# One hybrid block on one core: the adaLN sums in runs of sixteen products, eight buffers of raw weights

## The chip, the core and the metric

The kernel runs on one core of a Trainium2 chip. The metric is the device time of one execution in microseconds (us), from launch to end; lower is better. The engines are named as the profile names them: PE is TensorE, which multiplies matrices, and PEld its weight loads; DVE is VectorE, ACT ScalarE, POOL GpSimd; SP is SyncE, whose queue issues nearly all transfers, in order.

## What is computed

A single transformer-like block on 256 latent tokens and 256 context tokens of width 2048, in f32. Cut to what matters here:

```python
m_x = silu(c) @ ada_w + ada_b            # six vectors of 2048: shift1, scale1, gate1, shift2, scale2, gate2
m_c = silu(c_ctx) @ ada_w + ada_b
o_c, states = mix(rmsnorm(ctx) * (1 + m_c[1]) + m_c[0], zero states)   # w_in, then four recurrent mixers
o_x, _ = mix(rmsnorm(x) * (1 + m_x[1]) + m_x[0], states)
h = x + m_x[2] * o_x
h = h + m_x[5] * swiglu(rmsnorm(h) * (1 + m_x[4]) + m_x[3])
out = rmsnorm(h)
```

`mix` projects its input by `w_in` (2048 x 6816), runs four mixers (GLA, gated DeltaNet, a short gated convolution, RWKV-7), each forward and backward in chunks, and projects the result by `w_out`. The adaLN vectors 2, 3 and 4 (`gate1`, `shift2`, `scale2`) are needed only after the mixers. They are the sums that this case is about.

## The kernel before

**Order.** The program is written with a planner: each engine's order of instructions is laid out ahead of time from the order of the source, from costs that the planner assumes, and from priorities. Inside `with tc.high_priority()` an instruction is put ahead of the others as soon as the planner believes it is ready. On the chip each engine then takes its list strictly in that order. The units of the mixers stand in a hand-written list (`ORDER`, lines 41 to 44); lower-case tokens work on the context, upper-case ones on the latents.

**Stages of the span.** Up to about 159 us: norms, first adaLN vectors and an early part of the context's projection. 159 to about 1,100 us: mixers with their projections. Then `w_out`, the two SwiGLU matrices (to about 1,970 us) and the last norm.

**Projections in the mixers.** `proj` (line 596) makes one 128-column tile of `w_in` for 256 tokens. It goes in four parts (`hf`). Each part loads 128 x 512 numbers of `w_in` (256 KB) into a buffer `wraw`, splits them on ACT and DVE into a high half `wh` and a low half `wl` (`split`, line 253), and makes twelve products of 256 columns into the tile `big`, so 48 per call.

**The adaLN sums.** `ada_pieces` (line 285) makes the vector `ci` from 64 pieces (four blocks `j`, sixteen depth tiles `kt`) and a `finish`. A piece loads 256 KB of `ada_later` into a `wraw` and makes four products `ob<-wraw,sc`, of 32 columns of weights each, one for each quarter `g` of the output's partitions. In f32 a product is two passes of PE, so a piece is eight instructions in the trace. The three vectors' pieces and their three `finish` stand in a list `feed`. Each part `hf` of `proj` takes the first two entries (line 606), so a call of `proj` is mixed with eight pieces; 24 calls empty the list. Only the piece's load is at high priority; its products are not. The token `FF0` of `ORDER` runs what is left of the list.

**Buffers.** `wraw` has six buffers of 2 KB in each partition, used in turn by the loads of `w_in`, of `ada_later` and, later, of `w_out`, and by the row in `finish`. A load waits on SP's queue until the buffer six places earlier has been given back: after `wl` is made for one of `w_in`, after the four products for one of `ada_later`. `wh` and `wl` have three buffers each.

**Other tiles that the change touches.** `gdn` keeps the products of keys with keys in `gd_kk` (read in `front`) and of keys with queries in `gd_kq` (made and read in `mid`); `gla` keeps its transposed values in `gd_vt`. `short_conv` writes its result to `sc_y`, of two buffers, and `put_y` (line 886) makes the two halves `yH` and `yL` of it.

Of the kernel before, what the change touches and what calls it, by code (L numbers as in the profile page):

```python
# [16 lines left out]
P = 128  # L17
D = 2048
KT = D // P
# [156 lines left out]
def block_kernel(ctx: ExitStack, tc: tile.TileContext, x, cx, ada_first, ada_later, ada_b, w_in, w_early, w_out,  # L176
                 w_gu, w_down, final_g, consts, params, small, out):
    nc = tc.nc
# [9 lines left out]
    def mk(pool, shape, tag, bufs=None, dt=F32):  # L188
        pool = sub.get(tag[:3], pool) if pool is sub.get("mx") else pool
        return pool.tile(list(shape), dt, tag=tag, name=nm(tag), bufs=bufs)  # L190
# [10 lines left out]
    def tt(o, a, b, op, e=None):  # L201
        (e or V).tensor_tensor(out=o, in0=a, in1=b, op=op)  # L202
# [10 lines left out]
    def mm(o, l, r, start=True, stop=True):  # L213
        return TE.matmul(o, l, r, start=start, stop=stop)  # L214
# [7 lines left out]
    MUL, ADD, SUB, MIN, MAX = ALU.mult, ALU.add, ALU.subtract, ALU.min, ALU.max  # L222
# [4 lines left out]
    wpool = ctx.enter_context(tc.tile_pool(name="wpool", bufs=1))  # L227
# [17 lines left out]
    sc = mk(keep, [P, KT, 32], "sc")  # L245


    wp = [wpool, 512, 3, 6]

    def wraw():  # L250
        return mk(wp[0], [P, wp[1]], "wraw", wp[3])
# [33 lines left out]
    def ada_pieces(ci, bank_of, tmp):  # L285

        st = {}

        def piece(j, kt):
            if not st:  # L290
                st["ps"] = bank_of([P, 512])
            ps = st["ps"]
            with tc.high_priority():
                raw = wraw()
                rv = raw.rearrange("p (g c) -> p g c", g=4)
                r0 = (((ci - 2) * 4 + j) * KT + kt) * P
                nc.sync.dma_start(raw, ada_later[r0:r0 + P, :])
            for g in range(4):
                mm(ps[32 * g:32 * g + 32, j * P:(j + 1) * P], sc[:, kt, :], rv[:, g], kt == 0, kt == KT - 1)

        def finish():
            ps = st["ps"]
            row = wraw()
            if ci == 2:
                G.memset(row, 0.0)
                for g in range(4):
                    nc.sync.dma_start(row[32 * g:32 * g + 1, :], ada_b[0:1, ci * D + g * 512: ci * D + (g + 1) * 512])
                tt(row, ps, row, ADD)
                for g in range(4):
                    nc.sync.dma_start(gate_dram[0:1, g * 512:(g + 1) * 512], row[32 * g:32 * g + 1, :])  # L310
                return
            acopy(row, ps)
            pt = bank_of([P, 4, 4, 32])
            for b in range(4):
                TE.transpose(pt[:, b].rearrange("p a c -> p (a c)"), row[:, b * P:(b + 1) * P], ident)
            t = modB if ci == 3 else modA
            tt(t[:, 2, :].rearrange("p (g b) -> p g b", b=4), pt[:, :, :, 0].rearrange("p b g -> p g b"),
               pc("adab", ci * 16, 16).rearrange("p (g b) -> p g b", b=4), ADD)
            if ci == 4:
                stt(t[:, 2, :], t[:, 2, :], 1.0, pc("n2g", 0, 16), ADD, MUL)  # L320

        return [lambda j=j, kt=kt: piece(j, kt) for j in range(4) for kt in range(KT)] + [finish]

    def rstd_of(src, tmp, n):
        junk = mk(tmp, [P, D], "junk", 1)
# [60 lines left out]
    with ExitStack() as st:  # L386
# [93 lines left out]
        for i in range(1, NE):  # L480
            n, k = EARLY[i - 1]
# [30 lines left out]
    with mix:  # L512
# [83 lines left out]
        def proj(nHL, which):  # L596

            r0 = TIDX[which] * P
            H, L = nHL
            ps = PB([P, T], "big")  # L600
            for hf in range(4):
                with tc.high_priority():
                    raw = wraw()
                    nc.sync.dma_start(raw, w_in[r0:r0 + P, hf * 512:(hf + 1) * 512])
                    wh, wl = split(raw, V)
                for f in feed[:2]:
                    f()
                del feed[:2]
                for k in range(4):
                    kt = hf * 4 + k  # L610
                    a, b = wh[:, k * P:(k + 1) * P], wl[:, k * P:(k + 1) * P]
                    mm(ps, a, H[kt], kt == 0, False)
                    mm(ps, a, L[kt], False, False)
                    mm(ps, b, H[kt], False, kt == KT - 1)
            return ps

        def pcol(nHL, name, i):
            return proj(nHL, (name, i))

        def t1(tag, bufs=1):  # L620
            return mk(mx, [P, T], tag, bufs)
# [264 lines left out]
        def put_y(i, y):  # L886
            if not yt:
                A.dma_start(Y[i], y)
                parked.append(i)
                return  # L890
            acopy(yt[0][i], y)
            tt(yt[1][i], y, yt[0][i].bitcast(F32), SUB)
# [199 lines left out]
        def gdn(h, s, raw, sm):  # L1092
# [29 lines left out]
            def front():  # L1122
                cur[0] = "b"
                com.update(raw())
                k = cvs(com["k"], 1, "gd_k")
                v = cvs(com["v"], 2, "gd_v")
                l2(k, 1.0)
                tok = mk(mx, [P, 4, P], "gd_tok", 2)
                pt = PB([P, 4, P])
                for c in range(2):  # L1130
                    TE.transpose(pt[:, c], k[:, c * P:(c + 1) * P], ident)
                    TE.transpose(pt[:, 2 + c], v[:, c * P:(c + 1) * P], ident)
                acopy(tok, pt)
                pk = PB([P, 2, P])
                for c in range(2):
                    sl = slice(c * P, (c + 1) * P)
                    mm(pk[:, c], k[:, sl], k[:, sl])
                kk = mk(mx, [P, 2, P], "gd_kk", 1)
                V.tensor_copy(kk, pk)

                pbc = decays()
                dl = mk(mx, [P, 4, P], "gd_dl", 2)
                for d in range(2):
                    for c in range(2):
                        cs = sm["cum"][:, d, h, c:c + 1]
                        V.scalar_tensor_tensor(out=dl[:, d * 2 + c], in0=pbc[:, d, c * P:(c + 1) * P], scalar=cs,
                                               in1=dlm[d], op0=SUB, op1=SUB)
                act(dl, dl, AF.Exp, scale=-1.0)
                for d in range(2):
                    for c in range(2):  # L1150
                        u = d * 2 + c
                        stt(dl[:, u], kk[:, c], sm["nb"][:, d, h, c:c + 1], dl[:, u], MUL, MUL)
                com.update(kn=k, tok=tok, nL=dl, Xc=small_inverses(dl, lowers))

            def mid():
                cur[0] = "b"
                tok = com["tok"]
                R = com["R"] = mk(mx, [P, 4, 2, P], "gd_R", 1)
                for d in range(2):
                    for c in range(2):  # L1160
                        u = d * 2 + c
                        ts(R[:, u, 0], tok[:, c], sm["kes"][:, d, h, c:c + 1], MUL, e=G)
                if s == 0:
                    return
                k = com["kn"]
                q = cvs(com["q"], 0, "gd_q")
                l2(q, P ** -0.5)
                pk = PB([P, 2, P])
                for c in range(2):
                    sl = slice(c * P, (c + 1) * P)  # L1170
                    mm(pk[:, c], k[:, sl], q[:, sl])
                kq = mk(mx, [P, 2, P], "gd_kq", 1)
                V.tensor_copy(kq, pk)
                pbc = decays()
                for d in range(2):
                    for c in range(2):
                        cs = sm["cum"][:, d, h, c:c + 1]
                        stt(R[:, d * 2 + c, 1], pbc[:, d, c * P:(c + 1) * P], cs, atm[d], SUB, ADD)
                act(R[:, :, 1], R[:, :, 1], AF.Exp)
                qe = com["qe"] = mk(mx, [P, 2, T], "gd_qe", 1)  # L1180
                act(qe, pbc, AF.Exp)
                tt(qe, qe, bcast(q, 1, 2), MUL, e=G)
                for d in range(2):
                    tt(R[:, 2 * d:2 * d + 2, 1], kq, R[:, 2 * d:2 * d + 2, 1], MUL)
# [72 lines left out]
        def gla(p, s, raw, sm):  # L1257
# [18 lines left out]
            else:  # L1276
# [4 lines left out]
                for c in range(2):  # L1281
                    for hh in range(2):
                        TE.transpose(pt[:, c * 2 + hh], v[:, c, hh], ident)
            vt = mk(mx, [P, 4, P], "gd_vt", 1)
            V.tensor_copy(vt, pt)
            for d in range(2):
                pz = PB([P, T])
# [84 lines left out]
        def short_conv(t, nHL):  # L1372
            cc_ = t1("xs", 2)
            acopy(cc_, pcol(nHL, "c_c", t))
            pr = t1("xs", 2)
            tt(pr, pcol(nHL, "c_h", t), cc_, MUL)
            o = cc_
            conv(o, pr, [pc("scconv", tap * 4 + t) for tap in range(3)], 1)
            yo = t1("sc_y", 2)
            tt(yo, pcol(nHL, "c_b", t), o, MUL)  # L1380
            put_y(8 + t, yo)

        def rw(p, s):
            def raw():
# [291 lines left out]
```

## Time and profile before

| | us |
|---|---|
| median of 3 runs (1997.1 to 2002.27) | 2000.33 |
| the profiled execution, its own time | 1993.64 |
| its span, from first to last instruction | 1991.9 |
| PE busy in the span | 1896.2 |
| DVE busy | 1356.5 |
| ACT busy | 1023.8 |

The profiled execution is 6.7 us below the median, and its own time is 1.7 us over its span. PE's busy time counts each instruction from its start to the end of its results, and successive products overlap; what a product costs in a stream is read from the start of one to the start of the next.

### The profile page before, as it was taken

Reading aid. Unit: us, or ns where it says so; the run is one execution under the profiler, and the core shown is the slowest. Engines: PE = TensorE matmul, PEld = TensorE weight load, DVE = VectorE, ACT = ScalarE, POOL = GpSimd, SP = SyncE. Lnnn points to the kernel's source line nnn. Section 1 sums busy time; section 2 is a strip of 40 time slices with the busy share of each in tenths; the row PEclk is TensorE's granted clock in tenths of the full one; section 3 lists DMA queues with packets and bytes.
Section 4 is the critical chain, followed back from the end, with each engine's and each line's share of the span. In section 5 each row is a group of like instructions: output and inputs, shape, how many; then the busy total and the mean of one; then the engine's idle time right before and its main releaser. Section 6 shows DMA issues by size and latency. Waiting matters only on the chain.

```text
span 1991.9 us, 36160 instructions
## 1 busy us (share of the span) xinstructions
PE 1896.2 (95%) x13312; PEld 1624.0 (82%) x13312; DVE 1356.5 (68%) x3327; ACT 1023.8 (51%) x2125; POOL 160.0 (8%) x207
## 2 busy tenths in 40 slices
PE   5998999999999999999999998999999999999997
PEld 3776777787878888888998977888888888888886
DVE  4446856898877789899767566996555555555554
ACT  2225645566565555566455555455555555544443
POOL 0002000000001000101001001111001010000000
PEclk9999999999999999999999999999999999999999
DMA  8976685444367432222244665896555555565554
GB/s 347 403 302 214 218 264 186 128 129 153 98 207 230 146 106 67 91 77 74 93 160 146 211 189 183 291 323 229 187 189 183 189 186 185 202 210 192 194 196 149
DMA packets 162081, 374.66 MB, mean 188 GB/s; under 512 B 17896, under 2 KB 43752, under 8 KB 156784
## 3 DMA queue, kind: packets, MB, share of 16 engines
q1 hardware_dynamic: 156288, 368.21, 53.9%
q10 hardware_dynamic: 5616, 4.14, 0.7%
q8 instruction: 104, 1.70, 0.4%
q14 instruction: 73, 0.60, 0.1%
HBM read 360.48 MB, written 11.80 MB: 187 GB/s over the span
## 4 chain that ended last, share of the span: by engine, by line
PE 79%; DVE 10%; ACT 5%; DMA 4%; issue 2%; POOL 0%; SPq 0%; ACTq 0%; DVEq 0%; POOLq 0%
PE acc L214 40%; PE big L214 15%; PE la L214 6%; PE ea L214 5%; PE lb L214 4%; DVE wl L202 3%; PE eb L214 3%; PE ob L214 3%; ACT wh L197 2%; DMA wraw<-in_w_in 1%; DMA wraw<-in_ada_later 1%; PE pt L214 0%; ACT rw_z L193 0%; DVE ivaXc L202 0%; DVE ivaw L202 0%
## 5 line engine op out<-in xcount | busy, mean ns | idle before, releaser
L202 DVE TENSOR_TENSOR wl<-wraw,wh 128x512 fp32r<-128x512 f32 x856 | 569.2, 691 | 390.5 <-ACT wh L197 382.4
L197 ACT ACTIVATE wh<-wraw 128x512 fp32r<-128x512 f32 x856 | 510.0, 626 | 508.3 <-PE acc L214 193.9
L214 PE MATMUL acc<-n,wh 128*128 128x512 f32 x1408 | 494.1, 400 | 3.1 <-ACT wh L197 3.1
L214 PE MATMUL acc<-n,wl 128*128 128x256 f32 x1408 | 382.6, 282 | 0.3 <-DVE wl L202 0.3
L214 PE MATMUL big<-nh,wh 128*128 128x256 f32 x1056 | 315.9, 300 | 3.7 <-ACT wh L197 2.9
L214 PE MATMUL big<-nh,wl 128*128 128x256 f32 x1056 | 310.9, 295 | 1.3 <-DVE wl L202 1.3
L214 PEld LDWEIGHTS acc<-n,wh 128*128 128x128 f32 x1408 | 260.4, 189 | 59.6 <-ACT wh L197 3.4
L214 PE MATMUL big<-nl,wh 128*128 128x256 f32 x1056 | 306.8, 291 | 0.0
L214 PEld LDWEIGHTS acc<-n,wl 128*128 128x128 f32 x1408 | 268.2, 190 | 9.8 <-DVE wl L202 1.2
L214 PEld LDWEIGHTS big<-nh,wh 128*128 128x128 f32 x1056 | 199.7, 189 | 22.2 <-issue 12.5
L214 PEld LDWEIGHTS big<-nh,wl 128*128 128x128 f32 x1056 | 199.7, 189 | 7.8 <-issue 3.1
L214 PEld LDWEIGHTS big<-nl,wh 128*128 128x128 f32 x1056 | 199.8, 189 | 3.5 <-issue 2.9
L214 PE MATMUL acc<-wl,hH 128*128 128x512 f32 x352 | 137.2, 390 | 0.3 <-DVE wl L202 0.2
L214 PE MATMUL acc<-wh,hH 128*128 128x512 f32 x352 | 137.4, 390 | 0.0
L214 PE MATMUL acc<-wh,hL 128*128 128x512 f32 x352 | 137.0, 389 | 0.0
L214 PE MATMUL ob<-wraw,sc 128*32 128x128 f32 x1536 | 85.9, 286 | 10.8 <-DMA wraw<-in_ada_later 7.2
L202 POOL TENSOR_TENSOR hL<-sg,hH 128x256 fp32r<-128x256 f32 x44 | 47.4, 1078 | 451.3 <-ACT hH L197 451.3
L214 PEld LDWEIGHTS acc<-wl,hH 128*128 128x128 f32 x352 | 66.1, 188 | 15.1 <-DVE wl L202 1.4
L214 PEld LDWEIGHTS acc<-wh,hH 128*128 128x128 f32 x352 | 66.1, 188 | 13.9 <-ACT up L197 0.2
L214 PEld LDWEIGHTS acc<-wh,hL 128*128 128x128 f32 x352 | 66.1, 188 | 13.8
L214 PEld LDWEIGHTS ob<-wraw,sc 128*32 128x32 f32 x1536 | 39.0, 110 | 37.3 <-DMA wraw<-in_ada_later 11.2
L202 DVE TENSOR_TENSOR wl<-wr,wh 128x1408 fp32r<-128x1408 f32 x16 | 26.0, 1623 | 42.9 <-ACT wh L197 42.9
(483 smaller groups left out, 3169.3 us busy)
## 6 DMA issues: line engine op xcount, KB each, us to landing
wraw<-in_w_gu SPq DMA_DIRECT2D x174, 512.0 KB, 3.4
wraw<-in_w_in SPq DMA_DIRECT2D x264, 256.0 KB, 3.0
wraw<-in_ada_later SPq DMA_DIRECT2D x256, 256.0 KB, 4.0
wraw<-in_w_down SPq DMA_DIRECT2D x88, 512.0 KB, 4.2
ad<-in_ada_first SPq DMA_DIRECT2D x32, 1024.0 KB, 10.3
wraw<-in_w_out SPq DMA_DIRECT2D x64, 256.0 KB, 2.8
wr<-in_w_early SPq DMA_DIRECT2D x16, 704.0 KB, 6.2
xin<-in_cx SPq DMA_DIRECT2D x2, 1024.0 KB
```

Source lines behind the costliest of these rows:

```text
L197: A.activation(o, i, AF.Copy)
L202: (e or V).tensor_tensor(out=o, in0=a, in1=b, op=op)
L214: return TE.matmul(o, l, r, start=start, stop=stop)
```

## The change

The four pieces of four successive depth tiles become one entry, `run`. It first asks for all four loads, that of its first depth tile last, then lists the sixteen products (32 instructions), these now at high priority too. `proj` takes one entry at its first and third part, so it is still mixed with eight pieces. `feed` has 51 entries in place of 195. `wraw` has eight buffers. Room for the two more comes from sharing: `gd_kk`, `gd_kq` and `gd_vt` become one tile of 2 KB, the first two as its halves, and the short convolution's last product is written over its input in place of `sc_y`.

```diff
-    wp = [wpool, 512, 3, 6]
+    wp = [wpool, 512, 3, 8]
...
-        def piece(j, kt):
+        def run(j, k0):
+
             if not st:
                 st["ps"] = bank_of([P, 512])
-            ps = st["ps"]
+            ps, raws = st["ps"], {}
+            for kt in (k0 + 1, k0 + 2, k0 + 3, k0):
+                with tc.high_priority():
+                    raws[kt] = wraw()
+                    r0 = (((ci - 2) * 4 + j) * KT + kt) * P
+                    nc.sync.dma_start(raws[kt], ada_later[r0:r0 + P, :])
             with tc.high_priority():
-                raw = wraw()
-                rv = raw.rearrange("p (g c) -> p g c", g=4)
-                r0 = (((ci - 2) * 4 + j) * KT + kt) * P
-                nc.sync.dma_start(raw, ada_later[r0:r0 + P, :])
-            for g in range(4):
-                mm(ps[32 * g:32 * g + 32, j * P:(j + 1) * P], sc[:, kt, :], rv[:, g], kt == 0, kt == KT - 1)
+                for kt in range(k0, k0 + 4):
+                    rv = raws[kt].rearrange("p (g c) -> p g c", g=4)
+                    for g in range(4):
+                        mm(ps[32 * g:32 * g + 32, j * P:(j + 1) * P], sc[:, kt, :], rv[:, g], kt == 0, kt == KT - 1)
...
-        return [lambda j=j, kt=kt: piece(j, kt) for j in range(4) for kt in range(KT)] + [finish]
+        return [lambda j=j, k0=k0: run(j, k0) for j in range(4) for k0 in range(0, KT, 4)] + [finish]
...
-                for f in feed[:2]:
-                    f()
-                del feed[:2]
+                if hf % 2 == 0:
+                    for f in feed[:1]:
+                        f()
+                    del feed[:1]
...
-                kk = mk(mx, [P, 2, P], "gd_kk", 1)
+                kq = mk(mx, [P, 4, P], "gd_kq", 1)
+                kk = kq[:, 0:2]
...
-                kq = mk(mx, [P, 2, P], "gd_kq", 1)
+                kq = com["kq"][:, 2:4]
...
-            vt = mk(mx, [P, 4, P], "gd_vt", 1)
+            vt = mk(mx, [P, 4, P], "gd_kq", 1)
...
-            yo = t1("sc_y", 2)
-            tt(yo, pcol(nHL, "c_b", t), o, MUL)
-            put_y(8 + t, yo)
+            tt(o, pcol(nHL, "c_b", t), o, MUL)
+            put_y(8 + t, o)
```

## Rows read from the trace of the kernel before

**Rows 1.** The page, chain that ended last, by engine.

```profile
PE 79%; DVE 10%; ACT 5%; DMA 4%; issue 2%; POOL 0%; SPq 0%; ACTq 0%; DVEq 0%; POOLq 0%
```

**Rows 2.** Stretches: start:end, length, busy us (PE, PEld, DVE, ACT, POOL), clock, DMA share, GB/s.

```profile
161.00:163.00 2.00, 2.00 (x17) 1.76 (x20) 0.56 (x1) 0.92 (x2) 2.00 (x9) 0.50 0.79 217
...
170.00:300.00 130.00, 123.48 (x1268) 99.06 (x1268) 90.59 (x294) 72.44 (x158) 12.62 (x17) 1.00 0.76 246
300.00:400.00 100.00, 90.68 (x752) 72.61 (x750) 72.67 (x229) 55.29 (x135) 6.24 (x12) 0.93 0.49 154
400.00:575.00 175.00, 170.59 (x1486) 146.18 (x1486) 148.97 (x500) 106.66 (x243) 14.84 (x25) 1.00 0.42 134
575.00:627.00 52.00, 50.55 (x537) 38.27 (x536) 40.07 (x130) 27.45 (x63) 3.49 (x6) 1.00 0.79 259
627.00:1100.00 473.00, 454.07 (x3450) 421.08 (x3449) 392.28 (x1121) 270.99 (x593) 47.92 (x62) 1.00 0.33 110
```

**Rows 3.** Tile ob: count, ns min/median/max, first and last start.

```profile
L214 PE MATMUL ob<-wraw,sc x1536: 272/273/423, 159.6 to 626.4; 128*32 128x128 f32 x192
```

**Rows 4.** PE's timeline around one piece: start us, length, what.

```profile
186.93 0.28 PE L214 MATMUL big<-nh,wl 128*128 128x256 f32 x1
...
187.14 0.43 PE L214 MATMUL ob<-wraw,sc 128*32 128x128 f32 x8
187.50 0.39 PE L214 MATMUL big<-nh,wh 128*128 128x256 f32 x1
187.72 0.28 PE L214 MATMUL big<-nl,wh 128*128 128x256 f32 x1
```

**Rows 5.** PE's timeline around two pieces on end.

```profile
165.21 0.27 PE L214 MATMUL big<-nh,wl 128*128 128x256 f32 x1
165.41 0.64 PE L214 MATMUL ob<-wraw,sc 128*32 128x128 f32 x16
165.99 0.39 PE L214 MATMUL big<-nh,wh 128*128 128x256 f32 x1
166.21 0.28 PE L214 MATMUL big<-nl,wh 128*128 128x256 f32 x1
```

**Rows 6.** PE's timeline: the longest run, and one quarter of a piece.

```profile
576.92 1.29 PE L214 MATMUL ob<-wraw,sc 128*32 128x128 f32 x38
...
617.60 0.41 PE L214 MATMUL ob<-wraw,sc 128*32 128x128 f32 x2
617.94 0.70 PE L214 MATMUL eb<-gd_sq,ones 128*128 128x256 f32 x2
```

**Rows 7.** Waits, 155 to 630 us: who for whom, us in all, times, longest.

```profile
PE ob L214 <- DMA wraw<-in_ada_later: 7.2, 14, 2.4
...
SPq L297 <- PE ob L214: 102.4, 69, 11.7
SPq L604 <- PE ob L214: 58.0, 35, 23.2
```

**Rows 8.** SP's timeline: first and fifth load of w_in, eight of ada_later between.

```profile
250.92 0.37 SPq L604 DMA_DIRECT2D wraw<-in_w_in  x1
...
261.21 0.33 SPq L604 DMA_DIRECT2D wraw<-in_w_in  x1
```

**Rows 9.** The page, DMA issues: count, KB each, median us to landing.

```profile
wraw<-in_w_in SPq DMA_DIRECT2D x264, 256.0 KB, 3.0
wraw<-in_ada_later SPq DMA_DIRECT2D x256, 256.0 KB, 4.0
```

**Rows 10.** Tiles gd_vt and sc_y: instructions, ns min/median/max, first and last start.

```profile
L1285 DVE COPY gd_vt<-eb x4: 679/690/692, 395.6 to 1069.3; 128x512 f32<-128x512 f32 x4
...
L202 DVE TENSOR_TENSOR yL<-sc_y,yH x4: 418/419/426, 1068.9 to 1133.5; 128x256 fp32r<-128x256 f32 x4
```

**Rows 11.** PE's timeline: the first two runs; in brackets idle time before, and releaser.

```profile
159.57 0.64 PE L214 MATMUL ob<-wraw,sc 128*32 128x128 f32 x16 [3.50 <-ACT h_d_k L197]
...
162.76 1.08 PE L214 MATMUL ob<-wraw,sc 128*32 128x128 f32 x16
```

More of the change, by code (lines that the diff above doesn't have):

```diff
@@ L1152, in front @@
                         stt(dl[:, u], kk[:, c], sm["nb"][:, d, h, c:c + 1], dl[:, u], MUL, MUL)
-                com.update(kn=k, tok=tok, nL=dl, Xc=small_inverses(dl, lowers))
+                com.update(kq=kq, kn=k, tok=tok, nL=dl, Xc=small_inverses(dl, lowers))
             def mid():
```

## The prediction

> **What bounds the kernel now.** I read the page's chain first: PE holds 79% of the path that ended last [rows 1]. Then the span by stretches [rows 2]. The adaLN products start between 159.6 and 626.4 us [rows 3], so the change acts there, and there PE is busy for 91 to 98% of the stretches while DVE is busy for 70 to 85%. The reader should see two kinds of stretch. In 170 to 300 and 575 to 627 us the transfer engines are busy for 0.76 and 0.79 of the time; in 300 to 575 us for 0.42 to 0.49. I call them dense and thin. Third, PE's timeline, from the start of one product to the start of the next, because busy time hides the price of a switch between kinds of products. Last, the waits of SP's queue [rows 7]: loads stood 102.4 + 58.0 us for a buffer that adaLN products had not yet given back. PE itself stood only 7.2 us for adaLN data.
>
> **Price of a run of adaLN products.** Two projection products follow each other in 0.12 us: in [rows 4] one lies between the row at 186.93 and the eight. From 186.93 to 187.72 us there is one piece of eight instructions and two steps of the stream. 0.79 less 2 x 0.12 is 0.55 us for the piece. With two pieces on end [rows 5], 165.21 to 166.21 less 0.24 gives 0.76 us. So the second piece costs 0.21 to 0.22 us, and 0.33 us of the first is the price of going to the narrow products and back. The longest row bears this out: 38 instructions last 1.29 us against 0.43 for eight, 0.23 per further eight [rows 4, 6]. A quarter of a piece, two instructions, holds PE from 617.60 to 617.94, 0.34 us, where a whole piece holds it 0.36 [rows 4, 6]: a cut inside a piece costs as much as one between pieces.
>
> **How many runs.** Along PE's timeline, from the first start in [rows 3] to the last, I counted the unbroken runs of the 1,536 instructions: 165. 105 have two to eight instructions (57 whole pieces, 48 fragments), 59 have ten to sixteen, one has 46 (the 38 of [rows 6] and eight more). At 0.55, 0.77 and 0.55 + 5 x 0.22 = 1.65 us that is 57.8 + 45.4 + 1.7 = 104.9 us of PE's time, without waits. After the change there are 48 runs of 32 instructions: 0.55 + 3 x 0.22 = 1.21 us each, 58.1 us in all. **PE has 46.8 us less to do.** This takes the runs to be unbroken. I take that, since all sixteen products are urgent and the first cannot start before the last load; broken once each they would cost 48 x 0.33 = 16 us more.
>
> **What of it reaches the end.** The 192 pieces lie 117 in the dense stretches, 159 to 300 and 575 to 627 us, and 75 in the thin ones. By the same count the dense ones save 22 us of PE, the thin ones 25.
>
> Thin, 300 to 575 us: PE was busy 261 of 275 us, DVE 222 [rows 2]. With 25 us less DVE would stand at 222 / 250 = 0.89, against 392 / 473 = 0.83 in the stretch behind it, where PE is still 96% busy [rows 2]. So DVE does not become the bound outright, but chains through DVE will show more often. Bounds: nothing (chains take it all) to 25 us. I take 20, four fifths, nearer to the upper end because of that later stretch.
>
> Dense: a projection and its eight pieces need twelve loads of 256 KB, 3.15 MB. Before, one such round took 261.21 - 250.92 = 10.3 us [rows 8]. PE needs 48 x 0.12 + 2 x 1.21 = 8.2 us after the change. The transfer engines moved 246 GB/s at a share of 0.76 and 259 at 0.79 [rows 2], so some 325 GB/s if they were never idle, an estimate from these rows: 9.7 us for the round. So transfers, not PE, limit the gain to 0.6 us in each of 117 / 8 = 14.6 rounds, 9 us. Bounds: 22 us, if other work of the mixers spreads the loads; a loss, if the buffers are the limit. Eight buffers hold two thirds of a round. The run gives back four at a stroke; the last two loads of the next run go out after that, land 4.0 us later [rows 9], and the run takes some 1.0 us from its first start: with 0.7 us for two issues [rows 8] 5.7 us a half, 11.4 a round, 1.1 us over 10.3 and 16 us in 14.6 rounds. With 3.0 us to landing, as for `w_in` [rows 9], it is 9.4. I take 10 us of gain.
>
> **Other edits.** The wait on a load now stands before sixteen products, and behind it on PE's list are the projection's products and the mixers' chains. The loads themselves are as many and as large; a run's four go out together ahead of the next part's `w_in`, whose twelve products wait for it through ACT and DVE. That is in the round above. `gd_kk` and `gd_kq` are written and read by DVE alone, in its own order, so sharing adds nothing there. `gd_vt` is read by PE: the four copies into it [rows 10] keep their place, and at most two of the DeltaNet units behind a GLA unit must wait for its last product. The order puts the projections of other units between; uncovered it is a copy's length, 0.7 us, twice. The short convolution's result now holds its buffer until `yL` is made, 0.42 us by DVE [rows 10] and about as much by ACT, four times: 3.4 us if nothing covered it, at 1,067 us and later, where other products fill PE. I cost these at nothing and keep 5 us for the range. In the `w_out` and SwiGLU stages the loads and products stay the same, so I cost two more buffers at nothing there.
>
> **Sum.** 20 + 10 = 30 us off the profiled execution's 1993.6 gives 1963.6. That execution lies 6.7 us under the median of the runs, so against the median it is **1970 us**, 1.5% faster. About 0.3%, 6 us, is what a measurement of this kernel can tell from no change.
>
> **The rivals.** *All of it arrives.* The full 46.8 us, and part of the waits at narrow products: 1953 us, and 1940 if some 13 us of loads' waits go too. For it: SP's 160 us behind adaLN products, and the two added buffers. Against it: the share of 0.76 to 0.79. Chance 0.17.
>
> *Buffers still bind.* The dense stretches give nothing or lose up to 10, the thin ones 15: 1985 to 1995 us. For it: the 11.4 us round. Chance 0.19, of which 0.07 is no measurable change.
>
> *Slower: PE stands before each run.* PE takes its list in order; where the planner believes four loads landed before they have, PE stands with everything behind it. A piece waits for one load, a run for the last of four. It decides at 46.8 / 48 = 0.98 us per run. At 1.5 us the time is 2000 + 48 x 1.5 - 46.8 = 2025 us. For it: a load takes 4.0 us [rows 9], and the dense stretches leave little slack. Against it: the 14 waits came to 0.5 us each [rows 7], and eight buffers let the plan ask earlier. Chance 0.06.
>
> *The clock.* From 161 to 163 us the granted clock was 0.50, the lower of its two levels, 1.2 GHz [rows 2]. PE had stood 3.5 us before 159.57, and a run of sixteen that lasts 0.64 us at full clock lasted 1.08 [rows 5, 11]. If longer waits ahead of each run brought this back, 48 runs of some 1.08 us would each take 1.08 x 0.44 / 0.64 = 0.74 us more: 36 us returned, and 1990 us or more. Against it: the clock is 1.00 in both dense stretches, waits included [rows 2]. Chance 0.03, 0.02 of it no change or a small gain, 0.01 slower. The Trainium skill, "TensorE: Matmul & The Clock Gate", section "HAM oscillation — how this bites in real kernels", speaks against this change: where short groups of products alternate with waits for data, the array falls back to its slow rate each time. By that rule the time is this rival's, by the rows the sum's; the trace agrees only in that the clock fell in stretches with waits.
>
> **How the numbers follow.** The forecast, 1955 to 1985 us, has 0.55; everything arriving 0.17; buffers binding 0.19; PE standing 0.06; the clock 0.03. Faster by over 0.3%: 0.55 + 0.17 + 0.12 + 0.01 = 0.85. Within 0.3%: 0.07 + 0.01 = 0.08. Slower: 0.06 + 0.01 = 0.07. The range runs from 1942, inside "all of it arrives", to 1994, the edge of no change; it leaves out about 0.05 below and 0.14 above.
>
> **What would show it.** The timeline after should have some 48 runs of 32 instructions, each about 1.0 us from its first start to the next product; fragments of two or six would show the first step wrong. Waits of PE for `ada_later` should stay near 7 us; above 40 the third rival holds. SP's waits for adaLN products should fall under 160 us. The dense stretches' share should rise towards 0.85, with a round near 9.7 us; a round over 10.3 shows that the buffers bind. The span behind 627 us should be as long as before, within 5 us. A replanned order that lengthens the mixers' chains anywhere from 159 to 1,100 us would make the sum wrong without any of these terms being so.

## The result, and the profile after

The changed kernel takes **1976.78 us** in the median of four runs (1975.5 to 1979.17), against 2001.3 for the kernel before in the same comparison: ratio **0.988**, 95% interval 0.9861 to 0.99. That is 24.5 us faster. The forecast was 1970, 30 us faster, in a range of 1942 to 1994. The profiled execution of the changed kernel took 1979.17 us, at the upper end of its runs, and that of before 1993.64, under all of its runs, so the two traces show 14.5 us of the 24.5.

PE's timeline of the changed kernel around one run (start, length, what):

```profile
184.20 1.08 PE L214 MATMUL ob<-wraw,sc 128*32 128x128 f32 x32
185.22 0.38 PE L214 MATMUL big<-nh,wh 128*128 128x256 f32 x1
185.44 0.28 PE L214 MATMUL big<-nl,wh 128*128 128x256 f32 x1
```

Thirty-two instructions in 1.08 us; [rows 4, 5] gave 0.43 + 3 x 0.22 = 1.09. Along the timeline there are 44 such runs and two of 64, in place of 165. Priced as in the prediction they cost 44 x 1.21 + 2 x 2.09 = 57.4 us, 47.5 less than before. The page shows what the trace has of that; PE's busy time and the chain by engine, after:

```profile
PE 1858.0 (94%) x13312; PEld 1622.9 (82%) x13312; DVE 1352.5 (68%) x3327; ACT 1020.7 (52%) x2125; POOL 155.0 (8%) x207
...
PE 75%; DVE 9%; DMA 8%; ACT 5%; issue 2%; POOL 0%; SPq 0%; ACTq 0%; DVEq 0%; POOLq 0%
```

PE is busy 1896.2 - 1858.0 = 38.2 us less, and its idle time grew from 1991.9 - 1896.2 = 95.7 to 1977.4 - 1858.0 = 119.4 us, by 23.7. The difference is the 14.5 us. Busy time falls by less than the price said. Taken in each trace from the start of the product ahead of a run to the start of the one behind it, less PE's idle time and one step of 0.12 us, the 165 runs come to 94 us and the 46 to 56, which is 37 less. So the prices of the pieces, 104.9 us in all, were some 11 us too high. The chain's share of DMA doubled against [rows 1].

To see where, I cut both traces at the same amount of other work: at the 1,100th, 2,000th, 3,400th and 3,800th of PE's products other than `ob<-wraw,sc`. The kernel before reaches the last three at 320.5, 556.1 and 631.6 us, the changed one at 323.5, 547.8 and 615.7; the tables start 18.3 us behind the 1,100th. The stretches between, first of before, then of after (start:end, length, busy us of PE, PEld, DVE, ACT and POOL, clock, DMA share, GB/s):

```profile
167.00:320.50 153.50, 146.43 (x1470) 117.59 (x1469) 109.66 (x361) 84.66 (x188) 15.05 (x23) 1.00 0.73 235
320.50:556.00 235.50, 222.26 (x1906) 186.84 (x1905) 190.92 (x625) 139.66 (x325) 17.07 (x30) 0.97 0.44 139
556.00:631.60 75.60, 74.08 (x738) 58.60 (x739) 57.90 (x181) 42.75 (x94) 6.38 (x9) 1.00 0.70 229
```

```profile
170.50:323.50 153.00, 136.00 (x1526) 119.91 (x1527) 110.19 (x358) 87.89 (x203) 10.65 (x19) 0.99 0.79 257
323.50:547.80 224.30, 207.09 (x1947) 185.77 (x1947) 185.36 (x594) 129.62 (x301) 17.57 (x32) 0.98 0.48 152
547.80:615.70 67.90, 62.09 (x627) 55.87 (x626) 54.57 (x164) 42.37 (x94) 5.22 (x8) 0.97 0.63 199
```

The first, dense stretch is as long as before: PE has 10.4 us less to do in it and stands 9.9 us longer. The thin one is 11.2 us shorter, the last 7.7. The sums themselves also moved forward: from the 3,400th to the 3,800th product PE does 336 of their 1,536 instructions before and 224 after, 14 pieces fewer, and more of them in both stretches ahead. So the last stretch's 7.7 us are in part only work done earlier. Ahead of the change's place the traces differ by 3.5 us the other way (the 1,100th product at 148.7 and 152.2 us), and behind it the changed kernel loses 2 us up to the 7,500th.

Waits from 155 to 630 us, after (who for whom, us in all, times, longest), against [rows 7]:

```profile
PE ob L214 <- DMA wraw<-in_ada_later: 21.2, 21, 2.9
...
SPq L608 <- PE ob L214: 45.3, 27, 23.5
...
SPq L298 <- DMA wraw<-in_ada_later: 28.2, 21, 3.3
...
SPq L298 <- PE ob L214: 24.6, 48, 1.9
```

PE stands 21.2 us for adaLN loads in place of 7.2. SP's waits for adaLN products fell from 160.4 to 69.9 us, and those put down to the adaLN loads themselves rose from 7.5 to 44.1.

The chain that ended last, within the first of these stretches, before and after:

```profile
by line: PE big L214 30.1%; PE ob L214 13.0%; DMA wraw<-in_w_in 9.3%; PE la L214 7.9%; DMA wraw<-in_ada_later 6.7%; PE eb L214 4.3%; PE lb L214 4.1%; PE ea L214 3.6%; DVE wl L202 2.2%; ACT wh L197 2.1%; issue 1.4%; PE ea L993 1.4%; DVE smd 
```

```profile
by line: DMA wraw<-in_ada_later 40.1%; PE big L214 21.1%; PE ob L214 13.3%; DMA wraw<-in_x 5.6%; PE la L214 4.1%; DVE wl L202 2.2%; PE lb L214 1.6%; PE eb L214 1.6%; issue 1.5%; DVE ivbw L202 1.3%; PE ea L214 1.3%; DVE ivbXc L202 1.3%; ACT 
```

So after the change two fifths of that stretch, 61 us in 13 places of 3.9 to 5.8 us, lie in adaLN loads on the path, against 7% before.

The four runs shown start 5.7 us apart on average (PE's timeline). They are among the closer ones: from 171.7 to 322.0 us 22 runs start, and the median step is 6.3 us, 12.6 for a round of two runs.

```profile
177.83 1.08 PE L214 MATMUL ob<-wraw,sc 128*32 128x128 f32 x32
...
184.20 1.08 PE L214 MATMUL ob<-wraw,sc 128*32 128x128 f32 x32
...
189.66 1.08 PE L214 MATMUL ob<-wraw,sc 128*32 128x128 f32 x32
...
194.88 1.08 PE L214 MATMUL ob<-wraw,sc 128*32 128x128 f32 x32
```

From the first load of `w_in` to the fifth, as in [rows 8], the kernel before has ten rounds that begin from 163.9 to 285.4 us: 10.3 to 21.4 us, median 12.2. The 10.3 of [rows 8] is the shortest of them. The changed kernel has ten from 164.0 to 275.9: 10.3 to 17.3 us, median 11.9.

### The profile page after: what moved, and what is told of

Read it like the earlier page. It is cut to its first block, busy times and chain, and to the rows that moved or that the text cites. A ratio compares the mean times of both kernels' runs of the same rounds, so it can differ in the third digit from the quotient of the medians.

```text
span 1977.4 us, 36172 instructions
## 1 busy us (share of the span) xinstructions
PE 1858.0 (94%) x13312; PEld 1622.9 (82%) x13312; DVE 1352.5 (68%) x3327; ACT 1020.7 (52%) x2125; POOL 155.0 (8%) x207
## 4 chain that ended last, share of the span: by engine, by line
PE 75%; DVE 9%; DMA 8%; ACT 5%; issue 2%; POOL 0%; SPq 0%; ACTq 0%; DVEq 0%; POOLq 0%
PE acc L214 40%; PE big L214 14%; PE la L214 6%; DMA wraw<-in_ada_later 5%; PE ea L214 5%; PE lb L214 3%; DVE wl L202 3%; PE eb L214 3%; PE ob L214 2%; ACT wh L197 2%; PE pt L214 0%; DMA wraw<-in_x 0%; DMA xin<-in_cx 0%; ACT rw_z L193 0%; DMA wraw<-in_w_in 0%
## 5 line engine op out<-in xcount | busy, mean ns | idle before, releaser
L214 PE MATMUL big<-nh,wh 128*128 128x256 f32 x1056 | 311.9, 296 | 4.4 <-ACT xs L197 3.0
L214 PE MATMUL ob<-wraw,sc 128*32 128x128 f32 x1536 | 52.7, 280 | 24.9 <-DMA wraw<-in_ada_later 21.2
L202 DVE TENSOR_TENSOR wl<-wr,wh 128x1408 fp32r<-128x1408 f32 x16 | 26.0, 1624 | 43.3 <-ACT wh L197 43.3
```

## The experiments

Each is the changed kernel with one edit, timed against the kernel before on the same chip. Theory A: the gain is fewer switches, and what is missing was lost to the runs' loads. Theory B: what is missing was lost to the mixers' own chains (or, in the first run, the gain is the two buffers).

**Parts of the change.** Old pieces, eight buffers, sharing kept:

```diff
-        def run(j, k0):
+        def piece(j, kt):
...
-                if hf % 2 == 0:
-                    for f in feed[:1]:
-                        f()
-                    del feed[:1]
+                for f in feed[:2]:
+                    f()
+                del feed[:2]
```

> The changed kernel with the old pieces: eight buffers of raw weights and the shared tiles stay, the runs of four are undone. The narrow products are cut up as before, so PE has its 47 us back. Theory A (the gain is fewer switches between kinds of products; in the dense stretches it is eaten by the wait for four loads): 1990 to 2001 us, since a piece needs one load and eight buffers ask a little earlier. Theory B (the gain is the two buffers): 1977 us, as the changed kernel. PE waits for adaLN loads: 7 us or less in either.

Measured: 1992.69 us, ratio 0.9951 (0.9938 to 0.9964), in Theory A's range. The buffers are not the gain, but they are some of it.

The same with `wp = [wpool, 512, 3, 6]`, so that only the sharing of tiles is left:

> The kernel before with the sharing of tiles alone: old pieces, six buffers; the three tiles of the mixers are one and the short convolution's product is written in place. Theory of the prediction (the sharing costs nothing): within 4 us of the kernel before, so that the 10 us which the old pieces gained with eight buffers are the buffers'. Rival (a new plan by chance): 1990 to 1996 us without the buffers too.

Measured: 2000.32 us, ratio 0.9997 (0.9987 to 1.0008). The sharing neither costs nor brings anything, and PE's timeline has the same 165 runs. So 0.0046, 9 us, are the buffers' with old pieces.

Runs with six buffers, `wp = [wpool, 512, 3, 6]`:

> The changed kernel with six buffers in place of eight: runs of four alone. Theory A: a run holds four of six buffers, so a half round (two loads of w_in, four of ada_later) can overlap less; a half round goes from the 5.6 us of the changed kernel to some 6.5 to 7 us in the dense stretches, PE's waits for adaLN loads go from 21 us to 40 us or more, and the time is 1990 to 2005 us. Theory B (mixers' chains gave the gain back, not the loads): within 5 us of 1977.

Measured: 1982.4 us, ratio 0.9912 (0.9896 to 0.9928). The runs alone bring 17.6 us of the 24, the buffers 6 on top. Both theories missed: the time is under A's range, just outside B's, and PE's waits for adaLN loads are 17.4 us, not over 40.

**The order of the four loads.**

```diff
-            for kt in (k0 + 1, k0 + 2, k0 + 3, k0):
+            for kt in range(k0, k0 + 4):
```

> The changed kernel with the loads of a run in the order of its products: the first product's load is issued first, not last. Theory A: PE starts a run when one load has landed and then stands between pieces, inside the run, where the narrow products cannot give way; the waits move from before the run into it. If the planner cuts the runs, 10 to 16 us come back: 1980 to 1993 us. Rival (the order of the four loads does not matter, since all of them must land): within 4 us of 1977.

Measured: 2013.25 us, ratio 1.007 (1.0055 to 1.0084): slower than the kernel before by 14 us, and worse than either expectation. The timeline has 172 runs, 167 of them of eight instructions; PE's timeline of this kernel:

```profile
200.49 0.43 PE L214 MATMUL ob<-wraw,sc 128*32 128x128 f32 x8
...
201.51 0.43 PE L214 MATMUL ob<-wraw,sc 128*32 128x128 f32 x8
```

About four projection products stand between pieces. With the first load first, nearly every piece stands by itself and pays its switch: PE is busy 1901.3 us, 43.3 more than in the changed kernel, and the span is 33.5 us longer. (That the planner starts each piece as its own load is expected is how I read this; the plan's reasons are not in the trace.) The one line that puts that load last is worth 36 us by the medians, 38 by the ratios; with urgent products it is what keeps the runs whole.

**Runs of two.**

```diff
-            for kt in (k0 + 1, k0 + 2, k0 + 3, k0):
+            for kt in (k0 + 1, k0):
...
-                for kt in range(k0, k0 + 4):
+                for kt in range(k0, k0 + 2):
...
-        return [lambda j=j, k0=k0: run(j, k0) for j in range(4) for k0 in range(0, KT, 4)] + [finish]
+        return [lambda j=j, k0=k0: run(j, k0) for j in range(4) for k0 in range(0, KT, 2)] + [finish]
...
-                if hf % 2 == 0:
-                    for f in feed[:1]:
-                        f()
-                    del feed[:1]
+                for f in feed[:1]:
+                    f()
+                del feed[:1]
```

> The changed kernel with runs of two pieces, eight products, the first piece's load last; 96 runs, one at each part of a projection; eight buffers. By the price of the switches 96 runs of 0.77 us are 74 us, 16 more than 48 of 1.21. If only half of PE's time reaches the end, as for the runs of four: 1983 to 1987 us. If the shorter wait (two loads, not four) and the shorter block give back more than the switches cost: 1970 to 1977 us.

Measured: 1994.76 us, ratio 0.9974 (0.9961 to 0.9986), worse than expected. There are 90 runs, 87 of sixteen instructions, and PE's waits for adaLN loads are 22.0 us in 27 waits, against 21.2 in 21 with four: a wait for two loads is a little shorter, but there are more of them. The page:

```profile
PE 1874.5 (94%) x13311; PEld 1623.4 (81%) x13312; DVE 1356.7 (68%) x3327; ACT 1023.8 (51%) x2125; POOL 161.6 (8%) x207
```

PE is busy 16.5 us more than in the changed kernel, the 16 us of the price, and the span is 1994.0 us, 16.6 longer. By the ratios it is 19 us. Between these two kernels, both with urgent products, the whole price of the switches reached the end, and not half of it.

**Without the loads.** The runs, and then the pieces, multiply a resident tile:

```diff
-            for kt in (k0 + 1, k0 + 2, k0 + 3, k0):
-                with tc.high_priority():
-                    raws[kt] = wraw()
...
-                    rv = raws[kt].rearrange("p (g c) -> p g c", g=4)
+                    rv = sw[:, 0:512].rearrange("p (g c) -> p g c", g=4)
```

> The old pieces without their loads: the 192 loads of ada_later in the mixers are left out and every piece multiplies the same resident tile. Eight buffers, all for w_in. PE still has some 105 us of narrow products if they stand in 165 runs; without loads to wait for, the planner may place them otherwise. Theory A: 1975 to 1990 us. Together with the next kernel it gives the price of the switches without any wait for loads.

> The changed kernel without the 192 loads of ada_later: the runs of sixteen products multiply one resident tile. Theory A (loads eat some 20 us of PE's 47): the time falls to 1950 to 1960 us, and it lies 35 to 47 us under the kernel of pieces without loads. Theory B (chains through DVE and the new order eat them): 1970 to 1977 us, and at most 25 us under the pieces without loads.

Measured: pieces 1960.4 us, ratio 0.9793 (0.9779 to 0.9806); runs 1964.69, ratio 0.9816 (0.9803 to 0.983). The expectation that runs would be 35 us under pieces is plainly wrong; Theory A's 1975 to 1990 for the pieces and 1950 to 1960 for the runs both missed, and so did Theory B's 1970 to 1977. The pages, of the pieces first:

```profile
PE 1870.7 (95%) x13311; PEld 1620.1 (83%) x13312; DVE 1352.4 (69%) x3327; ACT 1021.1 (52%) x2125; POOL 157.8 (8%) x207
```

```profile
PE 1851.0 (94%) x13311; PEld 1625.6 (83%) x13312; DVE 1355.0 (69%) x3327; ACT 1020.9 (52%) x2125; POOL 161.3 (8%) x207
```

Their spans are 1962.0 and 1962.9 us, though PE has 19.7 us less to do in the runs, which the planner joined into three blocks of 512 instructions. That difference is worth nothing; in the medians the runs are 4.3 us slower.

**Priority.** Two theories were formed on this. C: an urgent, uncut run costs time because it goes ahead of the mixers' chains. D: the chains need their time whatever PE is relieved of.

```diff
-            with tc.high_priority():
+            if True:
                 for kt in range(k0, k0 + 4):
```

> The changed kernel with the sixteen products of a run at ordinary priority; the loads stay urgent. Theory C (half of PE's saving is lost because an urgent, uncut run of 1 us goes ahead of the mixers' chains, where a piece at ordinary priority waited for a moment in which PE had nothing better): the idle time of PE falls from 119 us of the span towards 105 and the time to 1962 to 1972 us, if the runs stay whole. Theory D (the mixers' chains need their time whatever PE is relieved of): within 4 us of 1977. If the planner cuts the runs up, as it did when the first load came first, PE gets some 20 us back and the time is 1985 to 1997 us.

> The runs without loads (one resident tile is multiplied in place of the loaded ones) with their products at ordinary priority, so that they differ from the pieces without loads only in how the list is cut. Theory C: the three blocks of 512 instructions come apart and fill PE's gaps, and the time is 1952 to 1962 us, as with the pieces without loads (1960) or under it. Theory D: 1963 to 1967 us, as with urgent products (1965).

Measured: with loads 1978.28 us, ratio 0.9889 (0.9873 to 0.9904); without them 1965.03, ratio 0.9824 (0.9808 to 0.984). D's numbers hold in both. C falls without the loads, where the blocks came apart into 97 runs and the time did not fall. With loads C was not put to its test, since the runs were cut into 103; the 1985 to 1997 us expected for cut runs missed, for it is as fast as the changed kernel. Its page:

```profile
PE 1875.6 (95%) x13311; PEld 1625.4 (82%) x13312; DVE 1351.6 (68%) x3327; ACT 1021.4 (52%) x2125; POOL 156.4 (8%) x207
```

PE is busy 17.6 us more than in the changed kernel, in a span of 1976.5 against 1977.4 us, and it stands only 5.8 us for adaLN loads, 15.4 less. So the added work took the place of idle time, most of it time in which PE had stood for loads.

**More buffers.** Twelve do not fit, so the tile of small matrices was cut in both of these, and its products take the wrong columns:

```diff
-    sw = mk(kp, [P, 3072], "sw")
+    sw = mk(kp, [P, 1024], "sw")
...
```

> The changed kernel with the tile of small matrices cut from 3072 to 1024 columns (its products read the wrong ones, so the output is not the reference's); eight buffers. It only makes room for the next kernel and is what that one is compared with. All theories: within 5 us of the changed kernel's 1977.

> The same with twelve buffers of raw weights. Theory A1 (in the dense stretches the half round is set by the way from four buffers given back to four loads landed): the half round falls from 5.6 us to the 4.8 us that the transfers need at 325 GB/s, PE's waits for adaLN loads fall from 21 us to under 10, and the time is 10 to 18 us under the kernel with eight. Theory A2 (the transfers themselves are the limit): within 5 us. Theory B (chains of the mixers): within 5 us, with fewer waits for loads.

Measured: eight 1982.29 us, ratio 0.9919 (0.9904 to 0.9934); twelve 1984.91, ratio 0.9928 (0.9916 to 0.9941). The kernel with eight was to be as fast as the changed one, and is 8 us slower by the ratios, 0.9919 against 0.988. It touches neither the runs nor their loads; PE's order differs from its 1,419th product on. Whether that order or the chip makes the 8 us is not shown. Differences of this size between the versions here are therefore not proof of a cause. Waits of the kernel with twelve:

```profile
PE ob L214 <- DMA wraw<-in_ada_later: 8.8, 9, 2.5
```

With eight they were 19.4 us, so the waits fell as A1 said, but the time did not. The median step between runs from 170 to 325 us fell from 6.25 us with eight to 5.6, not to 4.8. In the trace the kernel with twelve is 2.9 us ahead at the 3,800th product, 0.9 behind at the 7,500th and 5.4 behind at the 9,000th, in the SwiGLU stage. A1 falls at its size: more buffers bring the runs closer together, but of the 10 to 18 us some 5 at most appeared, and not at the end. Why the time behind the mixers grew is not shown.

**Runs spread out**, one in each projection:

```diff
-        "rw2:-150 PD0 PR0:-200 XX1 GD0:-100 RW0:50 PR1 PD3 PD1:150 RW1 FF0:-100 PR2:350 PR3:-750 "
+        "rw2:-150 PD0 PR0:-200 XX1 GD0:-100 RW0:50 PR1 PD3 PD1:150 RW1 PR2:350 PR3:-750 "
...
-                if hf % 2 == 0:
+                if hf == 0:
...
+        for f in feed:
+            f()
+        del feed[:]
         finish("b")
```

> The changed kernel with one run in each projection in place of two, and without the token that empties the list: the 48 runs are spread over 51 of the 66 projections, up to some 1,050 us, instead of 163 to 593 us. The same products, loads and buffers. Theory A (loads in the dense stretches ate 20 us): a round has eight loads, 2.1 MB, 6.5 us at 325 GB/s, against 6.9 us of PE's, so PE is the limit; the runs' waits fall under 8 us and the time to 1957 to 1967 us. Theory B (chains give it back): within 5 us of 1977.

Measured: 1981.33 us, ratio 0.9905 (0.9889 to 0.9921): B's number, though PE's waits for adaLN loads fell only to 13.3 us, not under 8. At the 3,800th product it is 45 us ahead of the kernel before, with more than half of the runs done, and at the 7,500th 13 us: the 22 runs that it had put off cost 32 us there, more than their price of 1.21 us each. No version here beats the changed kernel.

## Why the prediction was right

*The price and the number of runs: right for the runs, too high for the pieces.* 1.08 us of length for 1.09, 46 runs for 48. But of the 46.8 us off PE, 38.2 appear in its busy time: the 165 runs at 0.55 us and more were priced some 11 us too high. That the first load's place keeps the runs whole was stated as a reason, and the experiment on the loads' order shows it, at 36 us. (The prediction reads one product between the row at 186.93 and the eight in [rows 4]; in PE's timeline there is none. The sum needs two steps from 186.93 to 187.72, and has them.)

*The sharing at nothing: right* (0.9997). The buffers had no price of their own in the prediction; they are worth 9 us with pieces and 6 with runs, about the 8 us by which an edit without bearing on them moved the time.

*What reaches the end: the mis-sized term is the 20 us of the thin stretch.* The prediction took four fifths of 25 us there, for the reason that PE is still 96% busy in the stretch behind. The stretch got 11.2 us shorter, under half of the 25. The dense ones brought 0.5 + 7.7 = 8.2 us in the traces, against 10, and that agreement is luck. The 10 us stand on a round of 10.3 us before the change, which was the shortest of ten with a median of 12.2; the rounds hardly changed, and the gain came in the last stretch, where 14 pieces fewer were left to do.

Two pairs of kernels show that a saving of PE's time need not arrive: without loads, 19.7 us of PE's busy time between runs and pieces changed nothing, and with loads 17.6 us between urgent and ordinary products changed nothing. In the thin stretch PE was busy for 94% of the time and still had gaps. The reading that fits is that pieces at ordinary priority, as in the kernel before, stand in part in such gaps, where a count of starts charges them to the path and the path does not pay. It is a reading from pairs of kernels; which pieces of the kernel before stood in gaps that the path did not see is not shown. Urgent pieces behave otherwise: in runs of two 16.5 us more of PE's time cost 16.6 us, and with the first load first 43.3 cost 33.5.

*The loads: partly.* Without them the time is 1960 to 1965 us, 12 to 16 under the changed kernel, so the adaLN transfers still hold that much. That is an effect of all that goes with them: their waits, SP's queue, the `w_in` loads behind them, the transfers' share. In the first dense stretch they are on the path: 40% of the chain there, 7% before, for 3.9 to 5.8 us at a time. The prediction's own sign for "buffers bind", a round over 10.3 us, was no sign, since nine of ten rounds of the kernel before were over it; and its sum of 5.7 us for a half round is under the median step of 6.3. Twelve buffers brought the runs closer and left the time where it was. Which part of a load's way (the buffer given back, the queue, the transfer) holds the first dense stretch at 153 us stays open. The forecast that waits of PE would stay near 7 us was wrong (21.2), and the share rose to 0.79 in the first stretch, not to 0.85. Behind the 3,800th product the span is as long as forecast, within 2 us.

*The rivals.* "PE stands before each run" is refuted at its size: 21.2 us in 46 runs is 0.46 us each, under the 0.98 at which it decides. "The clock" did not decide: it is 0.97 to 0.99 in the three stretches, 0.97 to 1.00 before. "All of it arrives" did not happen: even with no loads at all the gain is 37 us in three blocks and 41 in pieces.

## What to carry to other kernels

Price a switch between kinds of products from start to start, then ask where the products stood and at what priority: here, of the 47 us counted over all pieces of an ordinary-priority list, about half arrived, while between urgent runs of two and of four all of it did. When several loads feed one block of products, let the first product need the load that is issued last; this planner then kept urgent blocks whole, and here that order decided between 24 us gained and 14 lost. A wait that gets shorter, as with twelve buffers, is no gain until the span says so. And time one version that should change nothing: here it moved by 8 us, which is the size of several effects above.

## What the runs showed of the hardware

The price of going to the narrow products and back, 0.33 us, did not depend on the run's length: from the first start to the next product are 0.36 us for eight instructions [rows 4], 0.58 for sixteen [rows 5] and 1.02 for thirty-two (184.20 to 185.22), 0.22 for each further eight.
